# Gate and up of three feed-forwards as 2x2 block products, and both state-space builds in one phase

## The chip, the cores and the metric

One core of a Trainium2 chip runs the whole program. The metric is device time in microseconds, from the first to the last instruction of one execution. Engines are called PE (TensorE), DVE (VectorE), ACT (ScalarE), POOL (GpSimd) and SP (SyncE, which issues most DMAs).

## What is computed

Two layers of a decoder trunk on one sequence of 512 tokens with 1024 features, all in float32. A layer has four phases, in this order: a gated feed-forward (ffn1), three token mixers side by side (mix), cross-attention to 256 memory tokens (att), a second gated feed-forward (ffn2).

```python
def swiglu_ffn(h, w_gate, w_up, w_down):        # 1024 -> 2816 -> 1024
    return (jax.nn.silu(h @ w_gate) * (h @ w_up)) @ w_down

for l in range(2):
    x = x + 0.5 * swiglu_ffn(rmsnorm(x, ffn1_norm[l]), ...)
    z = rmsnorm(x, mix_norm[l]) @ w_in[l]
    y = concat(s5_mixer(z[:384], ...), pool_mixer(...), conv_module(...))
    x = x + y @ w_out[l]
    x = x + cross_attention(rmsnorm(x, xattn_norm[l]), rmsnorm(mem, mem_norm[l]), ...)
    x = x + 0.5 * swiglu_ffn(rmsnorm(x, ffn2_norm[l]), ...)
return rmsnorm(x, final_norm)
```

The s5 mixer is a state-space scan over 24 groups; its matrices (powers of a complex diagonal, input and output matrices, phase tables) come from the parameters alone, not from x.

## The kernel before

**Layout.** Activations are feature-major: `xs` holds x as 8 tiles of 128 features by 512 tokens. PE multiplies in float32r, and every operand is split in two float32r parts, a high one (`xh`, `wh`: an ACT copy) and a low one (`xl`, `wl`: a DVE subtraction of the high part from the original). `mm3` (lines 235 to 238) makes each product of three matmuls: high·high, high weight·low activation, low weight·high activation.

**Weights.** `wload` (lines 223 to 230) fetches a 128x1024 tile by a DMA on SP's queue, copies it to `wh` on ACT (L227) and subtracts on DVE (L229). Each of raw, `wh` and `wl` has three buffers in the pool `wp`.

**Feed-forward.** `ffn` (line 255) walks 22 blocks of 128 hidden features. `gate_up(f)` makes gate and up of one block, each 8 feature tiles times three matmuls of 512 columns into one PSUM bank, then gates: two DVE products read PSUM and the token scale `rb` (L269, L273), ACT makes the sigmoid, two DVE products read SBUF (L274, L275), and `split` halves the result (L243, L245). The blocks come in groups of 6, 6, 5, 5; `down(p)` adds a group into the 8 outputs, and stands behind the first block of the next group. In the last feed-forward the last group runs token-major, so that tiles are normalised and stored one by one.

**Norms.** `Norm.add(kt)` (line 185) follows each finished x tile: ACT makes the scaled high part and the square, DVE the low part and the running sum (L183, L189). The token scale `rb` is needed only when a block is gated.

**State-space matrices.** `s5_build(l)` (line 362) is a generator. Each ffn1 steps it once a block (`next(bg, None)`), so each layer's matrices are built beside that layer's first feed-forward. Its wide products and sums run on POOL, with a few matmuls and transposes on PE. The matrices stay in SBUF (pool `cp`) until the mixer of their layer.

**Order.** The code is traced in program order; a scheduler lays out each engine's instructions ahead of time, by program order among those which its timing model takes to be ready. On the chip each engine then runs its list in order. Buffers in a pool that come under one tag are shared, and an instruction that writes into one waits until its readers are done.

Of the kernel before, what the change touches and what calls it, by code (L numbers as in the profile page):

```python
# [9 lines left out]
F32 = mybir.dt.float32  # L10
F32R = mybir.dt.float32r
# [33 lines left out]
def trunk_kernel(ctx: ExitStack, tc: tile.TileContext, io, out, phases=None):  # L45
# [43 lines left out]
    def vt(name, shape=(P, 512), dt=F32):  # L89
        return vp.tile(list(shape), dt, tag="V", name=name)  # L90
# [107 lines left out]

    def rsqrt_cols(acc, scale, name, mark=None):
# [35 lines left out]
    def mm3(ps, wh, wl, ah, al, first, last):  # L235
        T.matmul(ps, lhsT=wh, rhs=ah, start=first, stop=False)  # L236
        T.matmul(ps, lhsT=wh, rhs=al, start=False, stop=False)  # L237
        T.matmul(ps, lhsT=wl, rhs=ah, start=False, stop=last)  # L238
# [14 lines left out]

# [1 line left out]
    def ffn(which, l, norm, nxt, bg):  # L255
        wg, wu, wd = (io[f"{which}_w_{n}"][l] for n in ("gate", "up", "down"))
        rb = norm.rb()
        sizes = [6, 6, 5, 5]
        starts = [0, 6, 12, 17]
        gs = {}  # L260

        def gate_up(f):
            nm = f"{which}{l}_{f}"
            pg = mm(f"pg{nm}")
            proj(pg, wg, 0, f * P, norm.xg, f"g{nm}", split_w=pre.pop("gate", None))
            pu = mm(f"pu{nm}")
            proj(pu, wu, 0, f * P, norm.xg, f"u{nm}", split_w=pre.pop("up", None))
            a = bt(f"a{nm}")
            V.tensor_tensor(out=a, in0=pg, in1=rb, op=MUL)  # L269
            s = bt(f"s{nm}")  # L270
            A.activation(out=s, in_=a, func=AF.Sigmoid)
            u = bt(f"u{nm}")
            V.tensor_tensor(out=u, in0=pu, in1=rb, op=MUL)  # L273
            V.tensor_tensor(out=a, in0=a, in1=s, op=MUL)  # L274
            V.tensor_tensor(out=a, in0=a, in1=u, op=MUL)  # L275
            gs[f] = split(a, f"ff{nm}")

        def down(p):
            f0, n = starts[p], sizes[p]
            last = p == len(sizes) - 1  # L280
            for o in range(NK):
                ps = mm(f"pd{which}{l}_{p}_{o}")
                proj(ps, wd, f0 * P, o * P, [gs[f0 + i] for i in range(n)], f"d{which}{l}_{p}_{o}")
                V.scalar_tensor_tensor(out=xs[o], in0=ps, scalar=0.5, in1=xs[o], op0=MUL, op1=ADD)  # L284
                if last:
                    nxt.add(o)

        # last block: token-major, so that each token tile is normalised and stored while the next is computed
        xt, wt = {}, []
        fl, nl = starts[-1], sizes[-1]  # L290
# [46 lines left out]
        gain = []  # L337
        for p, (f0, n) in enumerate(zip(starts, sizes)):
            for i in range(n):
                gate_up(f0 + i)  # L340
                if i == 0 and p > 0:
                    down(p - 1)
                if nxt is None and f0 == fl:
                    if i == 0:
                        for h in range(2):
                            gain.append(st(f"fgain{h}"))
                            nc.sync.dma_start(out=gain[h], in_=io["final_norm"][h * 512:(h + 1) * 512].partition_broadcast(P))
                    else:
                        to_tokens(i - 1)
                    fetch_rows(i)  # L350
                next(bg, None)
        for _ in bg:
            pass
        if nxt is None:
            finish()
        else:
            down(len(sizes) - 1)

# [1 line left out]
    s5m = {}  # L360

    def s5_build(l):
# [44 lines left out]
        # powers of lambda, ascending 1..8 (pm) and descending 7..0 (pg)  # L407
# [4 lines left out]
        # z = (lambda - 1) / lam  # L412
# [21 lines left out]
        # unit phase of one chunk  # L434
# [9 lines left out]
        # input matrix (hat = [re; im], til = [-im; re]) and its product with z  # L444
# [11 lines left out]
        G.tensor_tensor(out=bbh, in0=bh, in1=zrb, op=MUL)  # L456
        G.tensor_tensor(out=tmp, in0=btl, in1=zib, op=MUL)
        G.tensor_tensor(out=bbh, in0=bbh, in1=tmp, op=ADD)
        G.tensor_tensor(out=bbt, in0=btl, in1=zrb, op=MUL)
# [527 lines left out]
    for i, (kind, l) in enumerate(phases):  # L987
        nxt = norm_for(i + 1)
        if kind == "ffn1":
            def bg():  # L990
                if l == 0:
                    yield from prepare()
# [30 lines left out]
```

## Time and profile before

| what | value |
|---|---|
| median of 2 runs | 2139.3 us (2138.47 to 2140.12) |
| profiled execution, span | 2138.3 us, 25180 instructions |
| PE busy | 2088.5 us, 98%, 9685 matmuls |
| DVE, ACT, POOL busy | 1301.8 us (61%), 751.5 us (35%), 441.7 us (21%) |
| mean granted clock of PE | 0.991 |
| HBM | 203.32 MB read, 6.29 MB written, 98 GB/s |

The phases follow each other on PE; their borders, read from the chain that ended last: ffn1 of layer 0 until about 398 us, its mixer to 602, attention to 712, ffn2 to 1081; ffn1 of layer 1 until about 1454 us, mixer to 1657, attention to 1775, ffn2 to the end. Matmuls are pipelined, so the duration of one (0.39 us for 512 columns) is longer than the distance at which the next one starts. "Idle before" in a row is the engine's idle time ahead of those instructions, with what ended it.

### The profile page before, as it was taken

The page shows a single profiled execution, that of the slowest core. Times are in us where ns is not written, and L with a number is a line of the kernel's source. Part 1 is how long each engine was busy: PE and PEld are TensorE (multiplying, and loading weights), DVE is VectorE, ACT ScalarE, POOL GpSimd, SP SyncE. Part 2 cuts the span into 40 slices and gives each one's busy share as a digit, 9 for nine tenths or more (in the row PEclk, how much of TensorE's full clock was granted, in tenths as well). Part 3 has the DMA queues.
Part 4 walks back from the last instruction along what each step waited for, and adds up shares of the span by engine and source line. Part 5 has one row for each costly group of instructions (what it writes and reads, how often), then busy time and mean ns, then how long its engine had stood idle before and what let it go on. Part 6 is the DMA issues. An engine that isn't in the chain of part 4 may idle for free.

```text
span 2138.3 us, 25180 instructions
## 1 busy us (share of the span) xinstructions
PE 2088.5 (98%) x9685; PEld 1733.4 (81%) x9685; DVE 1301.8 (61%) x1942; ACT 751.5 (35%) x1060; POOL 441.7 (21%) x477
## 2 busy tenths in 40 slices
PE   8999999989999999999999999999989999999998
PEld 6888888877787888888887888887868878888887
DVE  7766454699755544444577564456996655454454
ACT  4423222434434322222352323233344443222232
POOL 2217170457000000000013680006550000000000
PEclk9999999989999999999999999999999999999999
DMA  5342332444322323333333333334443323333241
GB/s 168 98 125 75 115 98 73 133 125 132 98 80 58 91 85 112 88 94 105 89 95 93 104 96 99 103 89 128 125 124 89 89 59 94 94 96 101 80 147 40
DMA packets 396256, 213.03 MB, mean 100 GB/s; under 512 B 31934, under 2 KB 387048, under 8 KB 396136
## 3 DMA queue, kind: packets, MB, share of 16 engines
q1 hardware_dynamic: 395344, 210.32, 33.8%
q8 instruction: 76, 1.25, 0.3%
q10 hardware_dynamic: 792, 1.10, 0.1%
q14 instruction: 44, 0.36, 0.1%
HBM read 203.32 MB, written 6.29 MB: 98 GB/s over the span
## 4 chain that ended last, share of the span: by engine, by line
PE 86%; DVE 10%; issue 1%; DMA 1%; ACT 1%; SPq 0%; POOL 0%; POOLq 0%; DVEq 0%; ACTq 0%
PE pgffn L236 7%; PE pgffn L237 7%; PE pgffn L238 7%; PE puffn L237 7%; PE puffn L238 7%; PE puffn L236 7%; PE pdffn L238 7%; PE pdffn L236 7%; PE pdffn L237 7%; DVE cacc L727 3%; PE qps L237 1%; PE po L236 1%; PE qps L236 1%; PE po L238 1%; PE pwo L236 1%
## 5 line engine op out<-in xcount | busy, mean ns | idle before, releaser
L236 PE MATMUL pgffn<-xh_ffn,wh_gffn 128*128 128x512 f32 x696 | 272.6, 392 | 0.0
L237 PE MATMUL puffn<-xl_ffn,wh_uffn 128*128 128x512 f32 x696 | 272.2, 391 | 0.0
L238 PE MATMUL puffn<-xh_ffn,wl_uffn 128*128 128x512 f32 x696 | 271.9, 391 | 0.0
L236 PE MATMUL puffn<-xh_ffn,wh_uffn 128*128 128x512 f32 x696 | 271.6, 390 | 0.0
L237 PE MATMUL pgffn<-xl_ffn,wh_gffn 128*128 128x512 f32 x696 | 271.4, 390 | 0.0
L238 PE MATMUL pgffn<-xh_ffn,wl_gffn 128*128 128x512 f32 x696 | 271.3, 390 | 0.0
L238 PE MATMUL pdffn<-h_ffffn,wl_dffn 128*128 128x512 f32 x664 | 257.9, 389 | 0.9 <-DVE wl_dffn L229 0.9
L237 PE MATMUL pdffn<-l_ffffn,wh_dffn 128*128 128x512 f32 x664 | 258.3, 389 | 0.0
L236 PE MATMUL pdffn<-h_ffffn,wh_dffn 128*128 128x512 f32 x664 | 257.8, 389 | 0.0
L227 ACT ACTIVATE wh_dffn<-wr_dffn 128x768 fp32r<-128x768 f32 (+1 forms) x120 | 94.9, 795 | 286.9 <-PE pdffn L237 148.3
L284 DVE SCALAR_TENSOR_TENSOR x<-pdffn,x 128x512 f32<-128x512 f32 x120 | 82.4, 689 | 168.7 <-PE pdffn L238 168.6
L273 DVE TENSOR_TENSOR uffn<-puffn,rb_ffn 128x512 f32<-128x512 f32 x88 | 60.7, 690 | 197.8 <-PE puffn L238 197.8
L227 ACT ACTIVATE wh_uffn<-wr_uffn 128x1024 fp32r<-128x1024 f32 x87 | 92.2, 1060 | 250.7 <-PE pgffn L237 155.2
L227 ACT ACTIVATE wh_gffn<-wr_gffn 128x1024 fp32r<-128x1024 f32 x87 | 92.2, 1060 | 249.5 <-issue 154.7
L269 DVE TENSOR_TENSOR affn<-pgffn,rb_ffn 128x512 f32<-128x512 f32 x88 | 60.7, 690 | 164.8 <-PE pgffn L238 158.6
L236 PEld LDWEIGHTS puffn<-xh_ffn,wh_uffn 128*128 128x128 f32 x696 | 131.0, 188 | 27.4 <-issue 0.2
L237 PEld LDWEIGHTS puffn<-xl_ffn,wh_uffn 128*128 128x128 f32 x696 | 131.0, 188 | 27.5 <-issue 0.2
L238 PEld LDWEIGHTS puffn<-xh_ffn,wl_uffn 128*128 128x128 f32 x696 | 131.0, 188 | 27.0
L238 PEld LDWEIGHTS pgffn<-xh_ffn,wl_gffn 128*128 128x128 f32 x696 | 130.7, 188 | 27.3
L237 PEld LDWEIGHTS pgffn<-xl_ffn,wh_gffn 128*128 128x128 f32 x696 | 130.8, 188 | 26.6
L236 PEld LDWEIGHTS pgffn<-xh_ffn,wh_gffn 128*128 128x128 f32 x696 | 130.7, 188 | 26.5
L238 PEld LDWEIGHTS pdffn<-h_ffffn,wl_dffn 128*128 128x128 f32 x664 | 124.6, 188 | 27.2 <-DVE wl_dffn L229 1.3
(456 smaller groups left out, 4197.4 us busy)
## 6 DMA issues: line engine op xcount, KB each, us to landing
wr_gffn<-in_ffn_w_gate_dram SPq DMA_DIRECT2D x87, 512.0 KB
wr_uffn<-in_ffn_w_up_dram SPq DMA_DIRECT2D x87, 512.0 KB
wr_dffn<-in_ffn_w_down_dram SPq DMA_DIRECT2D x64, 384.0 KB
wr_dffn<-in_ffn_w_down_dram SPq DMA_DIRECT2D x56, 320.0 KB
wr_k<-in_xattn_wk_dram SPq DMA_DIRECT2D x16, 512.0 KB
wr_v<-in_xattn_wv_dram SPq DMA_DIRECT2D x16, 512.0 KB
wr_wo<-in_w_out_dram SPq DMA_DIRECT2D x16, 512.0 KB
wr_q<-in_xattn_wq_dram SPq DMA_DIRECT2D x16, 512.0 KB
```

The costliest lines, as they stand in the source:

```text
L227: A.activation(out=h, in_=raw, func=AF.Copy)
L236: T.matmul(ps, lhsT=wh, rhs=ah, start=first, stop=False)
L237: T.matmul(ps, lhsT=wh, rhs=al, start=False, stop=False)
L238: T.matmul(ps, lhsT=wl, rhs=ah, start=False, stop=last)
L269: V.tensor_tensor(out=a, in0=pg, in1=rb, op=MUL)
L273: V.tensor_tensor(out=u, in0=pu, in1=rb, op=MUL)
L284: V.scalar_tensor_tensor(out=xs[o], in0=ps, scalar=0.5, in1=xs[o], op0=MUL, op1=ADD)
L727: V.scalar_tensor_tensor(out=acc[:, d:], in0=h[:, 0:S - d], scalar=cw[:, TAPS - 1 - d:TAPS - d], in1=acc[:, d:], op0=MUL, op1=ADD)
```

## The change

Three of the four feed-forwards (ffn2 of layer 0, ffn1 and ffn2 of layer 1) use a new function, `ffn7`. It takes two blocks of hidden features as a pair. Weights [2 halves of the features x 2 blocks] times activations [2 halves of the features x 2 halves of the tokens] is a product of 2x2 block matrices, made by seven block products instead of eight, with sums of blocks ahead and behind. A block product is 4 feature tiles times gate and up (z) times three matmuls, of 256 columns.

- Activation sums are made in the norm ahead (`PairNorm`, `combos`), each split in high and low, for two x tiles 512 features apart; the phases ahead finish x tiles in the order 0, 4, 1, 5, 2, 6, 3, 7.
- Weight sums (four a pair, 128x1024) are made on POOL (`wsum`), then split by `halves`.
- Three PSUM banks (x, y, z) collect; partial results are copied out (`keep`, ACT) or added (`out`, DVE) between products.
- `gated` works on both blocks of a pair, from SBUF, and is spread over the products that follow (`later`).
- `pipeline` writes the order: loads seven steps ahead, weight sums four, halves two. Groups are 6, 6, 6, 4 blocks.

The first feed-forward keeps `ffn`, and steps the background twice a block: it now builds the matrices of both layers. Layer 0 builds on POOL and keeps them in SBUF; layer 1 builds on DVE, spills them to DRAM, and its mixer loads them back. The small pools are merged into one of 53 buffers.

```diff
+    class PairNorm(Norm):
+        def add(self, kt):
+            self.sums(kt)
+            self.done.add(kt)
+            k = kt % HK
+            if {k, k + HK} <= self.done:
+                self.pair(k)
+        def pair(self, k):
+            xa = ct_(f"xa_{self.name}{k}", (P, 4, HS))
+            for h in range(2):
+                A.activation(out=xa[:, 2 * h:2 * h + 2, :], in_=xs[k + h * HK].rearrange("p (h t) -> p h t", t=HS),
+                             func=AF.Identity, scale=self.col(k + h * HK))
+            self.xg[k] = combos(xa, f"{self.name}{k}")
+    def combos(xa, name):
+        V.tensor_tensor(out=s1, in0=xa[:, 3, :], in1=xa[:, 1, :], op=SUB)
+        V.tensor_tensor(out=s3, in0=xa[:, 0, :], in1=xa[:, 1, :], op=SUB)
+        V.scalar_tensor_tensor(out=s2, in0=s1, scalar=-1.0, in1=xa[:, 0, :], op0=MUL, op1=SUB)
+        V.scalar_tensor_tensor(out=s4, in0=xa[:, 2, :], scalar=-1.0, in1=s2, op0=MUL, op1=SUB)
...
+    def halves(src, name, shape):
+        h = wp.tile(list(shape), F32R, tag="wh", name=f"wh_{name}")
+        A.activation(out=h, in_=src, func=AF.Copy)
+        lo = wp.tile(list(shape), F32R, tag="wl", name=f"wl_{name}")
+        V.tensor_tensor(out=lo, in0=src, in1=h.bitcast(F32), op=SUB)
+        return h, lo
+    def pipeline(steps, later, bg, per):
+        for i in range(-7, n):
+            if 0 <= i + 7 < n and steps[i + 7].load:
+                steps[i + 7].load()
+            if 0 <= i + 4 < n and steps[i + 4].mix:
+                steps[i + 4].mix()
+            if 0 <= i + 2 < n:
+                w[i + 2] = steps[i + 2].split()
...
+            while steps[i].after and later:
+                later.pop(0)()
+            steps[i].run(w.pop(i))
+            if steps[i].post:
+                steps[i].post()
+            if later:
+                later.pop(0)()
...
+    def ffn7(which, l, norm, nxt):
+        sizes = [6, 6, 6, 4]
+        def pair(f):
+            def load(kh, fh):
+                r = (ct_(f"wr_{nm}_{kh}{fh}", shape) if (kh, fh) == (0, 1) else
+                     wp.tile(list(shape), F32, tag="raw", name=f"wr_{nm}_{kh}{fh}"))
+                for z, w in enumerate((wg, wu)):
+                    nc.sync.dma_start(out=r[:, z], in_=w[...])
+            def wsum(i, a, b):
+                ts[i] = ct_(f"wt_{nm}_{i}", shape)
+                G.tensor_tensor(out=ts[i], in0=a, in1=b, op=ADD)
+            def run(c, i, first):
+                    for k in range(HK):
+                        xh, xl = norm.xg[k][i]
+                        for z in range(2):
+                            mm3(ps[c][:, z, :], w[0][:, z, k, :], w[1][:, z, k, :], xh, xl, first and k == 0 and z == 0,
+                                k == HK - 1, True)
+            def one():
+                    V.scalar_tensor_tensor(out=g, in0=g, scalar=sgn, in1=rb, op0=MUL, op1=MUL)
+                    A.activation(out=sg[0], in_=g, func=AF.Sigmoid)
+                    V.scalar_tensor_tensor(out=u, in0=u, scalar=sgn, in1=rb, op0=MUL, op1=MUL)
+            def two():
+                    V.tensor_tensor(out=g, in0=g, in1=sg[0], op=MUL)
+                    V.tensor_tensor(out=g, in0=g, in1=u, op=MUL)
+                    gs[f + b] = split(g, f"ff{nm}_{b}")
...
+            add("x", 1, True, lambda: raw[0, 0], lambda: keep("x", "u1"), lambda: load(0, 0))
+            add("z", 5, True, lambda: ts[5], lambda: keep("z", "u5"), lambda: load(0, 1),
+                lambda: wsum(5, raw[0, 0], raw[0, 1]))
+            add("x", 6, False, lambda: ts[6], lambda: keep("x", "u2"), lambda: load(1, 1),
+                lambda: (wsum(7, raw[1, 1], raw[0, 1]), wsum(6, ts[7], raw[0, 0])))
+            add("z", 3, False, lambda: raw[1, 1], lambda: out(1, 0, "z", "u2"))
+            add("x", 7, False, lambda: ts[7], lambda: out(1, 1, "x", "u5"), lambda: load(1, 0))
+            add("y", 2, True, lambda: raw[1, 0], lambda: out(0, 0, "y", "u1"))
+            add("x", 4, False, lambda: ts[4], last_post, None, lambda: wsum(4, ts[6], raw[1, 0]))
...
-    def s5_build(l):
+    def s5_build(l, kept):
+        E = G if kept else V
...
-                G.tensor_tensor(out=gt, in0=bc_m(bbh), in1=bc_p(pg, 0), op=MUL)
+                E.tensor_tensor(out=gt, in0=bc_m(bbh), in1=bc_p(pg, 0), op=MUL)
...
+        mats, rho, spill = s5m.pop(l)
+        if spill is not None:
+            for f in range(NS):
+                for i in range(len(MATS)):
+                    nc.sync.dma_start(out=mats[f][i], in_=spill[f][i])
...
-        for o in range(NK):
+        for o in (0, 4, 1, 5, 2, 6, 3, 7):
             ps = mm(f"pwo{l}_{o}")
```

## Rows read from the trace of the kernel before

**Rows 1.** The page: busy time of PE; the chain that ended last, by engine.
```profile
PE 2088.5 (98%) x9685; PEld 1733.4 (81%) x9685; DVE 1301.8 (61%) x1942; ACT 751.5 (35%) x1060; POOL 441.7 (21%) x477
...
PE 86%; DVE 10%; issue 1%; DMA 1%; ACT 1%; SPq 0%; POOL 0%; POOLq 0%; DVEq 0%; ACTq 0%
```
**Rows 2.** Busy time by stage; the first line names the columns.
```profile
core 0: us, PE busy (x) PEld busy (x) DVE busy (x) ACT busy (x) POOL busy (x), PEclk, DMA share, GB/s
...
398.00:570.00 172.00, 159.34 (x816) 132.91 (x815) 146.71 (x206) 68.41 (x92) 87.80 (x51) 0.94 0.39 117
712.00:1075.00 363.00, 363.00 (x1611) 300.79 (x1610) 184.83 (x237) 111.06 (x141) 1.01 (x1) 1.00 0.33 96
1090.00:1447.00 357.00, 354.79 (x1599) 293.77 (x1599) 218.95 (x354) 121.86 (x166) 118.82 (x174) 1.00 0.33 96
```
**Rows 3.** PE's waits over the span: who for whom, us, times, longest.
```profile
PE yps L681 <- DVE sy L677: 10.9, 4, 4.1
...
PE cps L474 <- DMA cn<-in_ssm_c_im_dram: 2.2, 1, 2.2
...
PE pdffn L238 <- DVE wl_dffn L229: 0.9, 1, 0.9
```
**Rows 4.** PE's timeline (start, duration), first and last of 24, 512 columns.
```profile
799.68 0.39 PE L238 MATMUL pdffn<-h_ffffn,wl_dffn 128*128 128x512 f32 x1
...
804.90 0.39 PE L237 MATMUL pdffn<-l_ffffn,wh_dffn 128*128 128x512 f32 x1
```
**Rows 5.** The same, first and last of 35, 256 columns.
```profile
1538.81 0.28 PE L238 MATMUL kps<-mg,wl_k 128*128 128x256 f32 x1
...
1542.89 0.28 PE L236 MATMUL kps<-mg,wh_k 128*128 128x256 f32 x1
```
**Rows 6.** DVE's groups by line and shape, 725 to 1075 us (busy, mean ns).
```profile
L229 DVE TENSOR_TENSOR wl_gffn<-wr_gffn,wh_gffn 128x1024 fp32r<-128x1024 f32 x22 | 26.8, 1220 | 4.1 <-ACT wh_gffn L227 4.1
...
L284 DVE SCALAR_TENSOR_TENSOR x<-pdffn,x 128x512 f32<-128x512 f32 x32 | 22.0, 690 | 50.9 <-PE pdffn L238 50.9
L229 DVE TENSOR_TENSOR wl_dffn<-wr_dffn,wh_dffn 128x768 fp32r<-128x768 f32 x16 | 15.3, 959 | 0.1
...
L275 DVE TENSOR_TENSOR affn<-affn,uffn 128x512 f32<-128x512 f32 x22 | 15.2, 690 | 0.5
L245 DVE TENSOR_TENSOR l_ffffn<-affn,h_ffffn 128x512 fp32r<-128x512 f32 x22 | 15.1, 688 | 7.0 <-ACT h_ffffn L243 7.0
```
**Rows 7.** ACT's groups, the same stretch.
```profile
L227 ACT ACTIVATE wh_gffn<-wr_gffn 128x1024 fp32r<-128x1024 f32 x21 | 22.3, 1062 | 66.1 <-issue 47.8 <-PE pdffn L237 17.5 <-ACT sq_ffn L179 0.5
...
L243 ACT ACTIVATE h_ffffn<-affn 128x512 fp32r<-128x512 f32 x22 | 13.9, 634 | 22.9 <-DVE affn L275 22.9
L271 ACT ACTIVATE sffn<-affn 128x512 f32<-128x512 f32 x22 | 13.6, 619 | 0.5 <-DVE affn L269 0.3
```
**Rows 8.** Timelines of POOL and DVE, 456 to 464 and 200 to 235 us.
```profile
458.37 2.37 POOL L229 TENSOR_TENSOR wl_k<-wr_k,wh_k 128x1024 fp32r<-128x1024 f32 x1
...
458.55 2.72 DVE L667 TENSOR_TENSOR sy<-sy,ssw 128x512 f32<-128x512 f32 x1
...
201.91 5.08 DVE L229 TENSOR_TENSOR wl_dffn<-wr_dffn,wh_dffn 128x768 fp32r<-128x768 f32 x1
...
202.02 0.46 POOL L545 TENSOR_TENSOR tab<-tab,ta 128x128 f32<-128x128 f32 x1
...
205.44 0.73 POOL L545 TENSOR_TENSOR tab<-tab,ta 128x256 f32<-128x256 f32 x1
```
**Rows 9.** DVE's groups, 1090 to 1440 us, while POOL builds.
```profile
L229 DVE TENSOR_TENSOR wl_gffn<-wr_gffn,wh_gffn 128x1024 fp32r<-128x1024 f32 x19 | 26.6, 1402 | 1.0 <-ACT wh_gffn L227 1.0
...
L229 DVE TENSOR_TENSOR wl_dffn<-wr_dffn,wh_dffn 128x768 fp32r<-128x768 f32 x16 | 22.0, 1372 | 0.1
...
L245 DVE TENSOR_TENSOR l_ffffn<-affn,h_ffffn 128x512 fp32r<-128x512 f32 x22 | 20.1, 915 | 5.8 <-ACT h_ffffn L243 5.8
```
**Rows 10.** POOL's groups, the same stretch.
```profile
L519 POOL TENSOR_TENSOR mout<-mout,mtt 128x512 f32<-128x512 f32 x6 | 10.9, 1842 | 0.0
...
L500 POOL TENSOR_TENSOR gt<-bbh,pg 128x512 f32<-128x512 f32 x6 | 7.6, 1272 | 41.0 <-PE vps L507 40.9
```

More of the change, by code (lines that the diff above doesn't have):

```diff
@@ L252, in proj @@
             mm3(ps, h[:, k, :], lo[:, k, :], ah, al, k == 0, k == n - 1)
[L255 to L280, printed above, removed]
-            for o in range(NK):
[L282 to L290, printed above, removed]
@@ new lines, in halves, with __init__ @@
+    def halves(src, name, shape):
+        h = wp.tile(list(shape), F32R, tag="wh", name=f"wh_{name}")
+        A.activation(out=h, in_=src, func=AF.Copy)
+        lo = wp.tile(list(shape), F32R, tag="wl", name=f"wl_{name}")
+        V.tensor_tensor(out=lo, in0=src, in1=h.bitcast(F32), op=SUB)
+        return h, lo
+    class Step:
+        def __init__(self, run, split, post=None, load=None, mix=None, after=False):
+            self.run, self.split, self.post, self.load, self.mix, self.after = run, split, post, load, mix, after
@@ new lines, in pipeline @@
+    def pipeline(steps, later, bg, per):
+        n = len(steps)
+        w = {}
+        for i in range(-7, n):
[5 more added lines that the diff above has]
+                w[i + 2] = steps[i + 2].split()
+            if i < 0:
+                continue
+            while steps[i].after and later:
[5 more added lines that the diff above has]
+                later.pop(0)()
+            for _ in range(per):
+                next(bg, None)
+        while later:
+            later.pop(0)()
+        for _ in bg:
+            pass
@@ L342, in ffn @@
                     down(p - 1)
[L343 to L351, printed above, removed]
+                for _ in range(2):
+                    next(bg, None)
@@ L484, in s5_build, with whole, half, put @@
         vsb = st(f"vsb{l}", (P, NG, GK))
+        def whole(name, shape):
+            return ct_(f"{name}{l}_{f}", shape) if kept else None
+        def half(tile_, sl, name, shape):
+            return sl(tile_) if kept else st(f"{name}{l}_{f}", shape)
+        def put(i, sl, t):
+            if not kept:
+                nc.sync.dma_start(out=sl(spill[f][i]), in_=t)
+        spill = None if kept else [[drp.tile(list(shape), F32, tag=f"m{f}{i}", bufs=1, name=f"sm{l}_{f}{i}")
+                                    for i, shape in enumerate(MATS)] for f in range(NS)]
         for f in range(NS):
-            minT = ct_(f"minT{l}_{f}", (P, GF, P))
+            minT = whole("minT", MATS[0])
             vps = ax(f"vps{l}_{f}", (P, GF, GK))
@@ L908, in attention @@
         out_head(NH - 1)
-        for o in range(NK):
+        for o in (0, 4, 1, 5, 2, 6, 3, 7):
             ps = mm(f"pwo{l}_{o}")
@@ L973, in norm_for, with seven @@
         kind, l = phases[i]
-        return Norm(f"{kind}{l}", lambda k: pc(gains[kind], l, k), G if i == 0 else V)
+        col = lambda k: pc(gains[kind], l, k)
+        if seven(i):
+            return PairNorm(f"{kind}{l}", col)
+        return Norm(f"{kind}{l}", col, G if i == 0 else V)
+    def seven(i):
+        return i > 0 and phases[i][0] in ("ffn1", "ffn2")
     cur = norm_for(0)
@@ L990, in bg @@
             def bg():
-                if l == 0:
+                if i == 0:
                     yield from prepare()
-                yield from s5_build(l)
-            ffn("ffn1", l, cur, nxt, bg())
+                    for k in range(L):
+                        yield from s5_build(k, k == 0)
+            if seven(i):
+                ffn7(kind, l, cur, nxt)
+            else:
+                ffn(kind, l, cur, nxt, bg())
         elif kind == "mix":
```

234 lines of the change are left out of this document (185 added, 49 removed).

## The prediction

> **What bounds the kernel now.** I read the page first. PE is busy 98% of the span and carries 86% of the chain that ended last [rows 1]. A busy PE need not be PE at its peak, so I asked for stages next. Through the last 363 us up to 1075 us, a whole feed-forward, PE is never idle, at a granted clock of 1.00 (the 2.4 GHz level), with VectorE (DVE) at 184.8 us and GpSimd (POOL) at 1.0 us. Layer 1's first feed-forward, in which the state-space matrices are built, has POOL at 118.8 us and DVE at 219.0 us, and PE idle for 2.2 us of 357 [rows 2]. The list of PE's waits agrees: in all feed-forwards one wait on a weight half (0.9 us) and one on a DMA (2.2 us); the long waits are the mixers' [rows 3], and there the granted clock falls to 0.94 [rows 2]. So in the feed-forwards only fewer PE columns, or a cheaper column, can shorten the run, and only while nobody else becomes later than PE.
>
> **PE's side of the change.** The price of a matmul is the distance between starts, not the duration. In steady runs 24 matmuls of 512 columns start 5.22 us apart, first to last: 0.227 us each [rows 4]. 35 matmuls of 256 columns with a new 128x128 weight each, as the change has them, start 4.08 us apart: 0.120 us each [rows 5]. Half the columns cost 53%, not 50%. Two blocks of gate and up took 2·2·8·3 = 96 matmuls of 512: 21.8 us. Seven products of 4·2·3 = 24 matmuls of 256 are 168: 20.2 us. That is 1.63 us less a pair; 11 pairs in each of three feed-forwards give 33·1.63 = **-53.8 us**. The down projections keep their columns. The Trainium skill ("TensorE: Matmul & The Clock Gate", Back-to-back issue gap) gives N/2.4 + 2.5 ns, 216 and 109 ns; by that the gain would be an estimated 33·2.37 = 78 us. Both rows here lie 11 ns above it, so its sum is not used.
>
> **What DVE, ACT and POOL get in exchange, per pair.** Prices are those of the stage in which POOL rests [rows 6, 7].
> - DVE: seven weight halves of 128x1024 at 1.22 instead of four: 8.5 us. Gating reads two SBUF tiles in all five steps for each of two blocks: 10·0.69 = 6.9 us (before, two of the five read PSUM). Three output sums of PSUM and SBUF: 3·0.69 = 2.1 us. Together 17.5 us in a pair that takes PE 20.2.
> - ACT: seven halves at 1.06, four PSUM copies, two sigmoids and two splits at 0.62 to 0.63: 12.4 us. It stays free.
> - POOL: four sums of two 128x1024 tiles. The nearest row, a two-input POOL instruction of that size, is 2.37 us [rows 8]: 9.5 us. POOL had nothing here before.
>
> DVE alone fits, with 2.7 us to spare. The question is whether DVE and POOL run beside each other. [rows 8] say no when the DVE instruction has two SBUF inputs: such a 0.69 us instruction, issued 0.18 us after a POOL sum, takes 2.72 us and ends after the sum does; elsewhere one of 0.96 us takes 5.08 us, through a chain of POOL instructions. Then a pair needs 8.5 + 6.9 + 9.5 = 24.9 us one after the other, and about 1.3 of the 2.1 us of PSUM sums that don't fall under a POOL sum: **26.3 us against PE's 20.2**, an excess of 6.1 wherever pair follows pair. The DVE halves are made two products ahead of PE, so PE waits for them; before, a pair was 21.8. By the Trainium skill ("SBUF — State Buffer", Who interferes with whom) the pair of ports is held for a whole instruction, which is this reading.
>
> The other reading is an average. In layer 1's first feed-forward 118.8 us of POOL lengthened the DVE's two-input work by about 22·0.18 + 16·0.41 + 66·0.21 = 24 us [rows 9], 0.2 us per us. By that a pair costs DVE 17.5 + 1.9 = 19.4 us and PE never waits. I don't take it: there two-input DVE work was about 120 us and POOL 119 us in 350 us, so they fitted beside each other in time. 24.9 us in 20.2 can't.
>
> **Where the excess lands.** A 6-block down projection is 8·18·0.227 = 32.7 us of PE and asks DVE for 8·(0.96 + 0.69) = 13.2 us and POOL for nothing. It can take the gating of the pair ahead of it (6.9 us), and in its last steps two halves and three POOL sums of the pair behind it (9.6 us), as the loads are issued seven products ahead. The order in a feed-forward is four pairs, down, three pairs, down, three pairs, down, one pair, down.
> - Four pairs: 4·6.1 = 24.5; less 6.9 and 9.6: 8.0. Bounds: 4.3 (all PSUM sums hidden and more prefetched) to 17.6 (nothing prefetched).
> - Three pairs, twice: 18.4 - 16.5 = 1.9 each (bounds 1.8 to 11.5).
> - The last pair: its excess is prefetched; but its last gating (about 5 us of DVE and ACT in turn) must end before the last down block; PE has 9 matmuls of three ready blocks for each of two outputs, 4 us: 2 (0 to 6).
> Sum 13.8 a feed-forward, three of them: **+41.4 us**.
>
> **The norm before a seven-product feed-forward.** For two feature tiles DVE now makes four sums, four low halves and two square sums, at most 0.69 each, some of half width: 5.6 us for two outputs. After attention two outputs are 2·8·3·0.227 = 10.9 us of PE against 9.4 us of DVE with weight halves and residual: only the last pair is late, 3 us, bounds 0 to 6. After the second feed-forward, whose last down has 4 blocks, two outputs are 5.4 us of PE against 8.4 us of DVE, four times: 12 less what PE can take from later products, 9, bounds 3 to 13. Attention twice and feed-forward once: **+15 us**. Before, PE didn't wait there at all [rows 2].
>
> **Both builds in the first feed-forward.** The matmuls, loads and small DVE steps only move. Layer 0's build stays on POOL at twice the rate per block. Layer 1's goes to DVE: 36 products and sums of 128x512 that took POOL 1.3 to 1.8 us [rows 10] take 0.69, 25 us; the other 66 us of POOL's 118.8 I put at half, 33 us (bounds 20 and 66). It is spread over 6 blocks of two background steps each: 9.7 us a block on top of the old 2·1.22 + 5·0.69 = 5.9, against 10.9 us of PE. Four blocks in a row have no down between them: 4·4.7 = 19, less weight halves made ahead and work that slides into the next down: **+10 us** (0 to 25). Its results go to DRAM and come back, 3 MB, ahead of the layer 1 mixer's weights on the SP queue; they can start while the last down runs: **+2** (0 to 8). The wait on the DMA in layer 1 goes: **-2.2** [rows 3].
>
> **Sum against the profiled execution:** 2138.3 - 53.8 + 41.4 + 15 + 10 + 2 - 2.2 = 2150.7. The median of the runs is 1.0 above the profile: **2152 us**.
>
> **The rivals.**
> - *PE's sum stands.* If the average reading holds, or the scheduler's order lets gating slide into the downs, the boundary and build terms vanish with it: 2139.3 - 53.8 - 2.2 = 2083. For it: PE has not one long wait in the feed-forwards now. Against: [rows 8]. It needs the whole added wait under 11 us.
> - *Nothing is made ahead.* One mechanism, on the other side: the raw weight tiles have three buffers, shared by pair and down, and SP's loads are in order. If the next pair's loads queue behind the down's, its POOL sums begin with its first product and block DVE just then; each stretch loses its 9.6 us again (6 for the last pair). 3·(3·9.6 + 6) = 104 us in full, 2256; with half of it, 2204. From the point where 30 us of the 104 are lost it is slower by 2%. Behind DVE's blocked half stand the output sums that free PE's accumulators, so PE would wait twice. For it: the pair's second load goes to another pool, its others don't; against: DMA is at a third [rows 2].
> - *ACT or DMA becomes the bound.* 12.4 of 20.2 us, and the weight bytes per us grow by 8%: I give it nothing.
>
> **Chances.** Ports in turn, with down as the relief: 0.51, 2152, its own range 2107 (low bounds) to 2182. PE's sum: 0.17, 2083. Nothing made ahead, half to all: 0.32, 2204 and up. The range must reach into both: 2083 to 2210 leaves out the upper part of the last. Two per cent, 43 us, is about what a measurement of this kernel can tell from no change: faster (under 2096) 0.17, the same 0.51, slower (over 2182) 0.32.
>
> **What the new profile would show.** Right: the 256-column products start 0.120 us apart inside a product and PE waits for `wl` halves on DVE at the ends of products, most in the first four pairs of a feed-forward; DVE's 128x1024 halves average well over 1.22 us there, and POOL's sums over 2.4; DVE and POOL together fill the pair stretches; the down stretches have no PE waits. A pair takes about 26 us in the middle of the first four. Wrong: pairs at 20.2 us with DVE halves near 1.3 (PE's sum), or PE waits in every pair behind a down too (nothing made ahead). If the products themselves start farther apart than 0.120 us, or the first feed-forward takes over 25 us longer than before, the error is in those terms.

## The result and the profile after

Median 2270.2 us (2 runs, 2269.3 to 2271.2), against 2139.3: a ratio of 1.061 (95% interval 1.0579 to 1.0641), 131 us slower. The forecast was no change that can be told, at 2152.

The page of the changed kernel, busy time of PE and the chain that ended last; they answer to [rows 1]:

```profile
PE 2081.9 (92%) x12061; PEld 1829.9 (81%) x12061; DVE 1690.0 (74%) x2376; ACT 929.0 (41%) x1331; POOL 720.9 (32%) x444
...
PE 57%; DVE 23%; issue 15%; ACT 2%; POOL 1%; DMA 1%; SPq 0%; DVEq 0%; POOLq 0%; ACTq 0%
```

Of the chain's "issue" (time in which the engine waited for nothing that the profile shows), 347 us, 222 lie in the two attention phases, whose length didn't change.

PE's busy time hardly fell: 2088.5 to 2081.9, 6.6 us, where 53.8 of work were taken away. Its idle time rose from 49.8 to 187.5 (span less busy). So there are two losses: waits (137.7 us more), and 47 us in which PE is busy without more work. The forecast had only waits, 68 us, half of those that came. Where they lie, by stage. The lines answer to [rows 2] and are cut at the last output matmul of each phase: first feed-forward, first mixer, feed-forward 2 of layer 0, feed-forward 1 of layer 1, attention of layer 1, the last feed-forward.

```profile
core 0: us, PE busy (x) PEld busy (x) DVE busy (x) ACT busy (x) POOL busy (x), PEclk, DMA share, GB/s
0.00:436.90 436.90, 399.32 (x1814) 326.44 (x1815) 309.51 (x716) 152.98 (x226) 126.91 (x197) 0.97 0.40 116
436.90:661.40 224.50, 191.81 (x945) 158.46 (x944) 165.51 (x234) 82.27 (x114) 91.87 (x53) 0.91 0.35 106
780.50:1160.00 379.50, 352.65 (x2406) 327.82 (x2404) 301.84 (x317) 170.39 (x230) 140.98 (x47) 0.98 0.32 92
1160.00:1536.30 376.30, 352.91 (x2380) 327.66 (x2381) 299.28 (x312) 164.78 (x219) 127.05 (x46) 0.97 0.35 107
1761.20:1880.40 119.20, 116.60 (x579) 97.71 (x578) 72.40 (x131) 54.02 (x102) 1.01 (x1) 1.00 0.25 72
1880.40:2269.30 388.90, 360.06 (x2424) 335.04 (x2423) 294.39 (x305) 167.49 (x228) 137.97 (x49) 0.97 0.30 90
```

Every stage has PE idle, attention only 2.6 us (2.3 before), and every stage but attention has a granted clock under 1.00. Phase by phase, by the same cuts in both traces:

| phase | before | after | change |
|---|---|---|---|
| first feed-forward | 391.1 | 436.9 | +45.8 |
| mixers, layer 0 and 1 | 201.4, 201.3 | 224.5, 224.9 | +46.7 |
| attention, twice | 119.3, 119.4 | 119.2, 119.2 | 0 |
| ffn2 of layer 0 and ffn1 of layer 1 | 734.7 | 755.8 | +21.1 |
| last feed-forward, to its last output | 364.5 | 382.3 | +17.8 |

PE's waits, which answer to [rows 3] (who for whom, us, times, longest). `wl_guffn` is the low half of a gate and up weight, `xm` a negated activation sum, `prm` and `affn` belong to the first feed-forward, `lsm` and `pq` to the mixers:

```profile
PE pxffn L281 <- DVE wl_guffn L302: 37.3, 23, 2.7
PE lmean L983 <- DVE lsm L981: 29.9, 2, 15.4
PE ppo L867 <- DVE pq L863: 18.1, 4, 7.8
PE pdffn L279 <- DVE affn L407: 8.2, 1, 8.2
...
PE pxffn L279 <- ACT xm_ffn L230: 5.9, 1, 5.9
PE puffn L279 <- DVE prm L651: 5.7, 1, 5.7
PE pdffn L281 <- DVE wl_dffn L272: 5.6, 1, 5.6
...
PE pxffn L280 <- DVE xm_ffn L231: 5.2, 1, 5.2
```

The first row is the wait that the prediction named, but not in the place that it named: the longest twelve of these waits, 1.91 to 2.70 us each, all stand at the first product of a pair. The mixers' two, 48 us, it didn't have at all. DVE's groups and then POOL's, 780 to 1536 us, which answer to [rows 6]:

```profile
L302 DVE TENSOR_TENSOR wl_guffn<-wt_ffn,wh_guffn 128x1024 fp32r<-128x1024 f32 x88 | 141.6, 1609 | 22.7 <-ACT wh_guffn L300 22.3
...
L494 DVE SCALAR_TENSOR_TENSOR guffn<-guffn,rb_ffn 128x512 f32<-128x512 f32 x44 | 54.4, 1235 | 0.7
```

```profile
L462 POOL TENSOR_TENSOR wt_ffn<-wr_ffn,wr_ffn 128x1024 f32<-128x1024 f32 x44 | 134.4, 3059 | 415.3 <-DMA wr_ffn<-in_ffn_w_up_dram 408.1 <-DVE l_ffffn L288 5.9 <-ACT u5ffn L477 1.2
L462 POOL TENSOR_TENSOR wt_ffn<-wt_ffn,wr_ffn 128x1024 f32<-128x1024 f32 x44 | 128.1, 2911 | 14.1 <-DMA wr_ffn<-in_ffn_w_up_dram 9.4 <-ACT wh_guffn L300 1.7
```

A half takes 1.61 us instead of 1.22, a gating step 1.24 instead of 0.69, a POOL sum about 3.0 instead of 2.37. How they lengthen each other is seen in the timelines of DVE and POOL (start, duration):

```profile
826.59 0.68 DVE L484 TENSOR_TENSOR guffn<-pzffn,u2ffn 128x512 f32<-128x512 f32 x1
827.19 2.82 DVE L302 TENSOR_TENSOR wl_guffn<-wt_ffn,wh_guffn 128x1024 fp32r<-128x1024 f32 x1
829.93 0.68 DVE L484 TENSOR_TENSOR guffn<-pxffn,u5ffn 128x512 f32<-128x512 f32 x1
830.65 2.18 DVE L494 SCALAR_TENSOR_TENSOR guffn<-guffn,rb_ffn 128x512 f32<-128x512 f32 x1
```

```profile
825.64 3.29 POOL L462 TENSOR_TENSOR wt_ffn<-wr_ffn,wr_ffn 128x1024 f32<-128x1024 f32 x1 [5.94 <-DVE l_ffffn L288]
829.01 6.09 POOL L462 TENSOR_TENSOR wt_ffn<-wt_ffn,wr_ffn 128x1024 f32<-128x1024 f32 x2
```

The half that starts at 827.19 gets nowhere until POOL's sum ends at 828.93, and then needs 1.1 us. The two sums with a PSUM input (0.68) pass beside POOL's sums unhindered. The gating step with two SBUF inputs waits again. This is the reading of [rows 8] that the prediction chose; the Trainium skill ("SBUF — State Buffer", Who interferes with whom) says that a DVE instruction with two SBUF inputs contends with a POOL instruction that reads SBUF, and calls the ports that they share an exclusive lock. These rows agree.

### The profile page after: what moved, and what is told of

Its sections match the earlier page's. It is cut to its first block, busy times and chain, and to the rows that moved or that the text cites. A ratio compares the mean times of both kernels' runs of the same rounds, so it can differ in the third digit from the quotient of the medians.

```text
span 2269.4 us, 31369 instructions
## 1 busy us (share of the span) xinstructions
PE 2081.9 (92%) x12061; PEld 1829.9 (81%) x12061; DVE 1690.0 (74%) x2376; ACT 929.0 (41%) x1331; POOL 720.9 (32%) x444
## 3 DMA queue, kind: packets, MB, share of 16 engines
q1 hardware_dynamic: 408896, 222.91, 33.1%
## 4 chain that ended last, share of the span: by engine, by line
PE 57%; DVE 23%; issue 15%; ACT 2%; POOL 1%; DMA 1%; SPq 0%; DVEq 0%; POOLq 0%; ACTq 0%
PE pdffn L279 6%; PE pdffn L281 6%; PE pdffn L280 6%; DVE wl_guffn L302 6%; DVE cacc L970 4%; PE pxffn L281 4%; PE pxffn L280 3%; PE pxffn L279 3%; PE pzffn L279 2%; PE pzffn L280 2%; PE pzffn L281 2%; PE pgffn L281 2%; PE pgffn L279 2%; PE pgffn L280 2%; PE puffn L279 1%
## 5 line engine op out<-in xcount | busy, mean ns | idle before, releaser
L462 POOL TENSOR_TENSOR wt_ffn<-wr_ffn,wr_ffn 128x1024 f32<-128x1024 f32 x66 | 203.7, 3091 | 601.5 <-DMA wr_ffn<-in_ffn_w_up_dram 587.4
L302 DVE TENSOR_TENSOR wl_guffn<-wt_ffn,wh_guffn 128x1024 fp32r<-128x1024 f32 x132 | 213.4, 1616 | 35.9 <-ACT wh_guffn L300 35.2
L281 PE MATMUL pxffn<-xh_ffn,wl_guffn 128*128 128x256 f32 x792 | 224.5, 284 | 2.3 <-DVE wl_guffn L302 2.3
L279 PE MATMUL pxffn<-xh_ffn,wh_guffn 128*128 128x256 f32 x792 | 224.9, 284 | 1.7 <-ACT u1ffn L477 1.4
L280 PE MATMUL pxffn<-xl_ffn,wh_guffn 128*128 128x256 f32 x792 | 224.3, 283 | 0.0
L462 POOL TENSOR_TENSOR wt_ffn<-wt_ffn,wr_ffn 128x1024 f32<-128x1024 f32 x66 | 192.4, 2915 | 19.3 <-DMA wr_ffn<-in_ffn_w_up_dram 13.1
L302 DVE TENSOR_TENSOR wl_guffn<-wr_ffn,wh_guffn 128x1024 fp32r<-128x1024 f32 x99 | 158.8, 1604 | 33.1 <-ACT wh_guffn L300 33.0
L279 PE MATMUL pzffn<-xh_ffn,wh_guffn 128*128 128x256 f32 x528 | 153.5, 291 | 8.2 <-ACT wh_guffn L300 4.5
L281 PE MATMUL pzffn<-xh_ffn,wl_guffn 128*128 128x256 f32 x528 | 152.3, 288 | 3.1 <-DVE wl_guffn L302 3.0
L281 PEld LDWEIGHTS pdffn<-h_ffffn,wl_dffn 128*128 128x128 f32 x672 | 127.1, 189 | 33.9 <-DVE wl_dffn L272 6.4
L280 PE MATMUL pzffn<-xl_ffn,wh_guffn 128*128 128x256 f32 x528 | 152.2, 288 | 0.0
```

Of the source, the lines that this page charges most:

```text
L279: T.matmul(ps, lhsT=wh, rhs=ah, start=first, stop=False, skip_group_check=skip)
L280: T.matmul(ps, lhsT=wh, rhs=al, start=False, stop=False, skip_group_check=skip)
L281: T.matmul(ps, lhsT=wl, rhs=ah, start=False, stop=last, skip_group_check=skip)
L302: V.tensor_tensor(out=lo, in0=src, in1=h.bitcast(F32), op=SUB)
L462: G.tensor_tensor(out=ts[i], in0=a, in1=b, op=ADD)
```

## The experiments

"Mixers" are always the lengths of layer 0 and layer 1; each run has its own runs of the kernel before beside it (2139.4 to 2139.7).

### Is it the pool, the builds or the feed-forwards?

**b_pool**: the kernel before, its three small pools merged as in the change, nothing else.

```diff
-    bp = ctx.enter_context(tc.tile_pool(name="bp", bufs=36))
-    vp = ctx.enter_context(tc.tile_pool(name="vp", bufs=4))
+    bp = ctx.enter_context(tc.tile_pool(name="bp", bufs=53))
-    ssp = ctx.enter_context(tc.tile_pool(name="ssp", bufs=13))
...
-        return vp.tile(list(shape), dt, tag="V", name=name)
+        return bt(name, shape, dt)
...
-        return ssp.tile(list(shape), dt, tag="S", name=name)
+        return bt(name, shape, dt)
```

> The kernel before, with its three pools of 36, 4 and 13 buffers merged into one of 53, and nothing else of the change. After the change each mixer took 23 us longer, in layer 0 too, where nothing of the mixer's code was changed. Theory M (the merged pool): the scheduler gives the mixer's state-space inputs their buffers later, and lists them behind convolution taps; then both mixers are 15 to 30 us longer here, 2170 to 2200 us in all, with the feed-forwards as before or a few us worse. Rival R (what the change does around the mixers, the spill or the norms): the mixers take 201 us as before, 2139 us. Where the first feed-forward also gets longer here, the pool has a part in that term too.

Measured: 2189.3 us, ratio 1.0231 (1.0201 to 1.0261). Mixers 225.6 and 224.2, the first feed-forward 389.2. That is the first theory's range: 50 us of the 131 come from lines without any arithmetic in them.

**b_build**: the kernel before, pools apart, with both builds in the first feed-forward, two steps a block, layer 1's on DVE and spilled, as in the change.

```diff
-                yield from s5_build(l)
+                    for k in range(L):
+                        yield from s5_build(k, k == 0)
...
-                next(bg, None)
+                for _ in range(2):
+                    next(bg, None)
```

> The kernel before, its pools apart as they were, with both layers' matrices built in the first feed-forward (two background steps a block, layer 1 on DVE, spilled and loaded back), and no seven-product feed-forward. Theory B (the builds): the first feed-forward becomes about 46 us longer, of which some 13 are matmuls that only move from layer 1's first feed-forward, which becomes shorter by that; the sum is +25 to +35, 2165 to 2175 us. Rival (the merged pool made the first feed-forward late): +13 there and -13 in layer 1, 2139 us within 8. The spill's load shows in the layer 1 mixer against that of layer 0: 0 to 8 us.

Measured: 2146.4 us, ratio 1.0033 (1.0021 to 1.0046). First feed-forward 407.0, +15.9; ffn2 and ffn1 of layer 1 721.9, -12.8, so most of it is work that moved, as the rival had it. Mixer of layer 1, which loads the spilled matrices, 202.1 against layer 0's 202.8: with the pools apart the loads cost nothing.

**b_poolbuild**: both edits together.

> The kernel before with both changes that b_pool and b_build made singly: one pool of 53 buffers, and both layers' matrices built in the first feed-forward; no seven-product feed-forward. Those two gave +50 and +7 us. If the terms only add, 2195 us, with the first feed-forward at 405 to 409 us. If they need each other (the builds' tiles and the feed-forward's now take buffers from one another), the first feed-forward is at 430 to 440 us as in the changed kernel, and the time 2215 to 2230. What is left to the changed kernel's 2270 us is the seven-product feed-forwards' own.

Measured: 2222.7 us, ratio 1.0384 (1.0354 to 1.0414). That is 83 us, 26 more than the two alone (50 and 7). The first feed-forward alone is 31 us longer than with the builds and the pools apart, 438.1 instead of 407.0; other phases give a little back. Layer 1's mixer takes 228.6 here, against 223.1 for layer 0's. Two windows of this kernel in that stretch, columns as above:

```profile
80.00:130.00 50.00, 30.77 (x118) 23.84 (x117) 43.19 (x146) 12.97 (x24) 27.30 (x35) 0.80 0.21 50
130.00:180.00 50.00, 45.01 (x207) 37.04 (x206) 32.09 (x26) 14.31 (x21) 39.40 (x77) 0.93 0.30 87
```

With the pools apart the same windows have PE busy 43.87 and 50.00 us. The changed kernel's are 31.77 and 44.37, the same loss. What remains for the seven-product feed-forwards is 2270.2 - 2222.7 = 48 us.

### Which of the merged pools?

**b_v** merges only the state-space tiles (tag S, 13 buffers) into the big pool; V, which holds the gated convolution inputs `ca` and `ch`, stays apart. **b_s** is the mirror.

```diff
-    bp = ctx.enter_context(tc.tile_pool(name="bp", bufs=36))
+    bp = ctx.enter_context(tc.tile_pool(name="bp", bufs=49))
-    ssp = ctx.enter_context(tc.tile_pool(name="ssp", bufs=13))
...
-        return ssp.tile(list(shape), dt, tag="S", name=name)
+        return bt(name, shape, dt)
```

> The kernel before, with the 13 small state-space buffers (tag S) merged into the big pool, 49 in all, and the 4 value buffers (tag V) left apart. Merging both cost 50 us, all in the two mixers (225.6 and 224.2 us against 201). Theory: it is the V tiles that do the harm. In the pool of one tag a value tile can take any buffer, and the scheduler then lets the value products and the pool mixer run ahead of the state-space scaling su; with 4 apart they can't. Then this run keeps both mixers near 203 us and takes about 2142. Rival: the S tiles do it, their quick turnover among 13 is lost and the chain su, yps waits for buffers held by long-lived B tiles. Then the mixers stay near 225 and the run takes about 2185. Halfway (mixers near 215, about 2165) would mean both.

> The mirror of the run with V apart: the kernel before, V merged into the big pool (40), the 13 S buffers apart. If V does the harm: mixers near 225 us, about 2185. If S does it: mixers near 203, about 2142. If each alone costs nothing and only the two together do, both runs come out near 2142.

Measured: b_v 2173.1 us (1.0122 to 1.0181), mixers 216.7 and 218.3; b_s 2157.7 (1.005 to 1.0109), mixers 211.5 and 210.1. Neither theory: each half costs, 33 and 18 us, and 51 together against b_pool's 50. Where, is read from two tiles in layer 0's mixer: `su`, the state-space input, and `lsm`, the sum of the convolution's outputs (count, duration in ns min/median/max, first and last start). First the kernel before, then b_v, then b_s:

```profile
L585 DVE TENSOR_TENSOR su<-psu,rb_mix x3: 1128/1134/1139, 425.4 to 438.1; 128x512 f32<-128x512 f32 x3
...
L738 DVE TENSOR_TENSOR lsm<-lsm,cv x1: 680/680/680, 545.1 to 545.1; 128x512 f32<-128x512 f32 x1
```

```profile
L584 DVE TENSOR_TENSOR su<-psu,rb_mix x3: 1108/1140/1142, 457.9 to 466.8; 128x512 f32<-128x512 f32 x3
...
L737 DVE TENSOR_TENSOR lsm<-lsm,cv x1: 693/693/693, 543.6 to 543.6; 128x512 f32<-128x512 f32 x1
```

```profile
L584 DVE TENSOR_TENSOR su<-psu,rb_mix x3: 1064/1125/1169, 423.1 to 436.7; 128x512 f32<-128x512 f32 x3
...
L737 DVE TENSOR_TENSOR lsm<-lsm,cv x1: 693/693/693, 551.6 to 551.6; 128x512 f32<-128x512 f32 x1
```

Merging S makes the state-space chain 29 us later and leaves the convolution; merging V makes the convolution 6.5 us later and leaves the state space. In b_pool both are late (454.1 and 564.6). DVE's work in layer 0's mixer is the same before and after, 167.3 and 165.5 us: only the order differs. Which buffer's release moves an instruction back was not separated.

**a_v4**: the changed kernel with V's four buffers apart again (49 and 4).

> The changed kernel with the four buffers for the mixer's convolution inputs and the attention's probabilities apart again (49 and 4 in place of 53). Theory: with one pool, the inputs of the second and third convolution tile find no buffer until the pooling mixes have freed theirs, so their matmuls stand behind the pooling's in PE's list; then the mixers go back to 201 to 207 us, and the time to 2225 to 2238. If the 13 buffers of the state-space tiles were what counted, the mixers stay over 220 us.

Measured: 2251.0 us, 19 less than the change, mixers 218.7 and 216.2. Neither branch came (201 to 207, or over 220): V's four buffers are a part of it, and the rest stays, as b_v has it.

**a_ssmfirst**: the changed kernel with the state-space input traced ahead of the pool mixer.

```diff
-        for i in range(NPL):
-            pool_mix(i)
         for f in range(NS):
             ssm_in(f)
+        for i in range(NPL):
+            pool_mix(i)
```

> The changed kernel with one block of the mixer moved: the state-space inputs are traced ahead of the pooling mixes, so that they ask for their buffers first. Theory M: both mixers lose most of their extra 23 us, 2225 to 2250 us in all. If buffers are not what makes the state-space inputs late, the mixers stay at 224 us and the time at 2270.

Measured: 2264.6 us, mixers 222.4 and 221.6. Written order alone gives back 6 us. The last scaling `su` of layer 0's mixer starts at 483.0 instead of 503.3 us, but the pool mixer's last `pq` then comes 13 us later (509.3), and the last `lsm`, for which PE waits 17.0 us there, is as late as before (611.0 against 611.3). The merged pool isn't mended by moving one step.

### What do the weight sums cost the feed-forwards?

**a_nosum**: the changed kernel in which each weight sum is replaced by one of its raw blocks; PE, ACT and DVE do as much as before.

```diff
-                ts[i] = ct_(f"wt_{nm}_{i}", shape)
-                G.tensor_tensor(out=ts[i], in0=a, in1=b, op=ADD)
+                ts[i] = b
```

> The changed kernel without POOL's weight sums: each product takes one of the raw blocks in place of the sum, so those products are not of the reference. Theory P (POOL's sums and DVE's two-input instructions take turns at the ports): the DVE weight halves fall from 1.61 to about 1.22 us, a pair that follows a pair takes 20.2 to 20.8 us instead of 22.3 to 23.4, and the three feed-forwards lose 40 to 70 us of waits in all; the boundary behind an x tile's norm shrinks too; 2200 to 2230 us. Rival (DVE's own load of 17.5 us a pair, or the accumulators' copies, hold PE): pairs stay over 22 us and the time over 2255.

Measured: 2192.0 us, 78 less than the change. ffn2 and ffn1 709.6, last feed-forward 349.2: 46.2 and 33.1 less, more than the 40 to 70 expected. DVE's half in its groups, 780 to 1490 us:

```profile
L302 DVE TENSOR_TENSOR wl_guffn<-wr_ffn,wh_guffn 128x1024 fp32r<-128x1024 f32 x153 | 186.8, 1222 | 78.1 <-ACT wh_guffn L300 76.4 <-DMA wr_ffn<-in_ffn_w_up_dram 1.7
```

1.22 us again. PE's timeline of a stretch of three pairs, its first matmul and the first of the down projection behind it; the change first, with the starts of its second and third pair, then this run:

```profile
912.92 0.28 PE L279 MATMUL pxffn<-xm_ffn,wh_guffn 128*128 128x256 f32 x1
...
933.07 0.28 PE L279 MATMUL pxffn<-xm_ffn,wh_guffn 128*128 128x256 f32 x1
...
954.32 0.28 PE L279 MATMUL pxffn<-xm_ffn,wh_guffn 128*128 128x256 f32 x1
...
977.43 0.40 PE L279 MATMUL pdffn<-h_ffffn,wh_dffn 128*128 128x512 f32 x1
```

```profile
899.76 0.28 PE L279 MATMUL pxffn<-xm_ffn,wh_guffn 128*128 128x256 f32 x1
...
960.24 0.40 PE L279 MATMUL pdffn<-h_ffffn,wh_dffn 128*128 128x512 f32 x1
```

60.5 us without sums: exactly three pairs at 168 times 0.120. With sums the pairs take 20.2, 21.3 and 23.1. All stretches, read in this way:

| stretch | PE's work | with sums | without |
|---|---|---|---|
| four pairs, in ffn2, ffn1, ffn2 | 80.6 | 99.9, 107.0, 102.6 | 84.8, 97.4, 84.8 |
| three pairs, six times | 60.5 | 64.5, 66.1, 66.1, 66.7, 66.2, 66.3 | 60.4 to 60.5 |
| the down projections between | 32.7 | 32.6 to 32.7 | 32.6 to 32.7 |

**a_dvesum**: the same sums, made on DVE.

```diff
-                G.tensor_tensor(out=ts[i], in0=a, in1=b, op=ADD)
+                V.tensor_tensor(out=ts[i], in0=a, in1=b, op=ADD)
```

> The changed kernel with the weight sums on DVE in place of POOL. Theory P (turns at the ports): a sum then costs DVE about 1.22 us in place of 2.4 to 3 us of POOL during which DVE's two-input instructions stand still; a pair asks DVE for 17.5 + 4.9 = 22.4 us, and pairs behind pairs take 22 to 23 us, pairs behind a down 20.2; the seven-product feed-forwards get 15 to 45 us shorter in all, 2225 to 2255 us. Rival (PE waits because a sum is late, whoever makes it, and DVE's list is full): no shorter, 2265 us or more.

Measured: 2243.5 us, 27 less than on POOL; in the feed-forwards 16.2 and 14.7 less.

```profile
L302 DVE TENSOR_TENSOR wl_guffn<-wt_ffn,wh_guffn 128x1024 fp32r<-128x1024 f32 x88 | 107.2, 1218 | 14.6 <-ACT wh_guffn L300 14.5
...
L462 DVE TENSOR_TENSOR wt_ffn<-wt_ffn,wr_ffn 128x1024 f32<-128x1024 f32 x44 | 53.5, 1215 | 0.2
```

Four more instructions of 1.22 us a pair on the busiest helper are cheaper than the same work on a resting engine: a pair then has 17.5 + 4.9 = 22.4 us in a row instead of 24.9, and in the middle of a stretch pairs start 21.7 us apart (PE's products come in a slightly different order there, too). The busy times by the page:

```profile
PE 2078.1 (93%) x12061; PEld 1824.0 (81%) x12061; DVE 1665.3 (74%) x2508; ACT 935.5 (42%) x1331; POOL 323.7 (14%) x312
```

DVE runs 132 instructions more than in the change and is busy 24.7 us less. With a_nosum's 1222 ns this puts the place at the ports. The rival, that a sum is late whoever makes it, fails in the change's own trace too: the twelve longest waits stand before a product of a raw block, which needs no sum, and ahead of the one that ends at 1054.72 DVE has no idle time for 17 us.

### The first feed-forward, and all repairs together

**a_rate**: the changed kernel, background at one step a block for ten blocks, then three.

```diff
-                for _ in range(2):
+                for _ in range(1 if f0 + i < 10 else 3):
                     next(bg, None)
```

> The changed kernel with the background stepped once a block in the first ten blocks of the first feed-forward and three times in the rest, in place of twice in all. The waits there stand at 84 to 145 us, in layer 0's build. If two steps a block of layer 0's build on POOL are their cause, the first feed-forward falls from 437 to 408 to 418 us and the time to 2240 to 2252. If the merged pool's buffers are, it stays over 428 us, or the waits move to the later blocks.

Measured: 2260.5 us, 10 less, the first feed-forward 423.4 instead of 436.9, between the two branches (418, 428); layer 0's mixer is 4 us longer. Its windows where the change lost most:

```profile
80.00:130.00 50.00, 50.00 (x224) 41.01 (x224) 39.83 (x162) 18.11 (x25) 2.42 (x7) 1.00 0.34 102
130.00:180.00 50.00, 50.00 (x231) 41.36 (x230) 31.10 (x30) 17.83 (x29) 28.72 (x34) 1.00 0.41 108
```

PE is full there now. What lengthens DVE's row in the change is seen in its timeline, the build's tiny products (24 elements a partition), and in POOL's, whose build steps follow each other there without a gap:

```profile
116.73 0.17 DVE L621 TENSOR_TENSOR prm<-prm 128x24 f32<-128x24 f32 x1
116.84 1.06 DVE L616 TENSOR_TENSOR prm<-prm 128x24 f32<-128x24 f32 x1
...
119.02 1.24 DVE L620 TENSOR_TENSOR ph<-prm 128x24 f32<-128x24 f32 x1
```

```profile
116.73 2.23 POOL L751 TENSOR_TENSOR mtt<-ctil,pm 128x512 f32<-128x512 f32 x2
118.92 2.55 POOL L752 TENSOR_TENSOR mout<-mout,mtt 128x512 f32<-128x512 f32 x2
```

An instruction of 0.17 us takes 1.1 to 1.2, and such a chain stands ahead of `affn`, for which PE waits 8.2 us. Before the wait of 5.6 us two halves `wl_dffn`, 0.96 us each alone, take 10.57 us together under POOL's chain. That isn't the whole cause: with the pools apart (b_build) the tiny products of 80 to 150 us last 27.8 us against 36.5, and PE has one wait there, 6.1 us. What else the merged pool puts ahead of `affn` was not separated.

**a_best**: the changed kernel with a_v4, a_dvesum and a_rate at once.

> The changed kernel with three repairs at once: value buffers apart (alone -19 us), weight sums on DVE instead of POOL (alone -27), and the background at one step a block in the first ten blocks, three after (alone -10). If the three act in different stretches (mixers; seven-product feed-forwards; first feed-forward), they add up: 2270.2 - 19.3 - 26.7 - 9.7 = about 2215, with PE idle near 145 us instead of 187.5. If they share one cause (buffers of the merged pool), less than the sum: 2225 to 2240. Either way it stays above the kernel before, 2139, since the sums still cost DVE 1.2 us each and the first feed-forward still builds twice.

Measured: 2212.3 us, ratio 1.0335 (1.0305 to 1.0365); first feed-forward 421.3, mixers 219.3 and 219.7. The three gains add up (58.0 against 55.7), as separate causes would. PE's idle time is 124.6 us by the trace, less than the 145 expected. It is still 73 us slower than the kernel before. No variant of the change that was run beats the kernel before; seven-product feed-forwards with all pools apart were not tried.

## Why the prediction was wrong

**PE's saving: right.** 0.120 us a matmul inside a product, 60.5 us for three pairs, so -53.8 stands. The formula of the Trainium skill ("TensorE: Matmul & The Clock Gate", Back-to-back issue gap), 109 ns, is given there for an isolated matmul; this stream lies above it, so the prediction was right not to use it.

**The sum.** The forecast missed by 118 us. Two steps failed most: the merged pool was put at nothing, and the relief in the pair stretches was too large. By the terms below, in us: the merged pool in the mixers 47, the builds 23, the pair stretches 40, the norm boundaries 10, less 2 for the spill. The last pair's 2 us held: PE waits 1.6 us for its gating in each of the first two seven-product feed-forwards.

**The merged pool: a term that was missing.** The change's description has the line, the sum gave it nothing. It cost 46.7 us in the two mixers, two fifths of the error, and 31 in the first feed-forward by way of the builds (438.1 against 407.0).

**Both builds: +10 in the forecast, 33 in the run** (45.8 less the 12.8 that left layer 1's feed-forward). The prediction's own sign for it, over 25 us longer, came. The place was wrong too. The prediction put it on layer 1's build on DVE in the late blocks; there PE is full but for 3.3 us from 230 to 437. It is layer 0's build, at 80 to 180 us. With the pools apart and the same builds the net cost is 3 (15.9 less 12.8), so the price of moving them was not the error; the pool was. The spill's +2 was 0 there.

**The pair stretches: mechanism right, size wrong.** From the table: with less without sums, the four-pair stretches lost 15.1, 9.6 and 17.8, predicted 8.0 each; the six three-pair stretches 4.0 to 6.2, 33 in all, predicted 1.9 each. Together 75 against 35. The step that failed is the relief: pairs took 20.2, 21.3, 23.1, so one pair behind a down is free, and the next two pay. The relief of 16.5 us a stretch was summed up as if DVE could spend it anywhere. And pairs behind pairs took 20.7 to 24.6 us, not 26.3: the excess for each was too high, the number of pairs that pay too low. One reason for the first is that DVE was priced by durations, not by the distance between starts, as PE was. With POOL at rest DVE's steps start 0.60 us apart where they last 0.68 (at 933.89, 934.50 and 935.10 us) and 1.13 where a half lasts 1.21 (935.10, then 936.23). By these starts the 24.9 us are an estimated 7.9 + 6.0 + 9.5 = 23.4. The lower clock, below, is part of the 75.

**The norm boundaries: +15 in the forecast, 25 measured.** Without sums the four-pair stretches exceed PE's work by 4.2, 16.8 and 4.2 (predicted 3, 9, 3). Behind attention the step held within 1.2 us; between two feed-forwards it was half of what came, and in the changed kernel PE waits there for `xm` twice, 5.9 and 5.2 us.

**PE's clock: not priced.** ffn2 and ffn1 should have had PE busy for 721.8 us (b_poolbuild) less 35.9; they had 705.6, 19.7 more; the last feed-forward in the same way 13.4 more. Windows and a timeline show the larger part. The first window lies behind one wait of 2.70 us; the other two, and the timeline, behind another of 2.70 us:

```profile
957.40:960.60 3.20, 3.18 (x26) 3.18 (x27) 3.20 (x5) 0.37 (x1) 0.00 (x0) 1.00 0.44 121
1054.70:1057.90 3.20, 3.18 (x15) 3.18 (x16) 3.20 (x5) 0.00 (x0) 0.00 (x0) 0.50 0.41 123
1058.10:1061.80 3.70, 3.70 (x33) 3.70 (x33) 3.56 (x5) 2.59 (x4) 0.00 (x0) 1.00 0.00 0
```

```profile
1054.72 0.58 PE L281 MATMUL pxffn<-xm_ffn,wl_guffn 128*128 128x256 f32 x1 [2.70 <-DVE wl_guffn L302]
...
1055.32 0.41 PE L280 MATMUL pxffn<-xm_ffn,wh_guffn 128*128 128x256 f32 x1
1055.53 0.41 PE L281 MATMUL pxffn<-xm_ffn,wl_guffn 128*128 128x256 f32 x1
```

Behind the wait that ends at 1054.72 the next 15 matmuls start 0.21 us apart at the 1.2 GHz level, then 0.12 at 2.4 again: it cost 1.4 us more. The equal wait that ends at 957.42 cost nothing more, at a granted clock of 1.00. Of the twelve waits of 1.91 to 2.70 us seven were followed by matmuls at the lower level and five weren't; what decides it, these runs don't show. [rows 2] had the sign of it, a granted clock of 0.94 where the mixer waits, and the prediction didn't turn it into a price. For the three feed-forwards over b_poolbuild: PE's work -53.8, idle time +72.1 (50.2 and 21.9), busy time beyond the work +33.1. That adds up to the 51.4 by which the two stages grew (33.9 and 17.5), by definition, as the 33.1 is what is left. Of it the lower clock is about 21: half of PE's busy time while the trace has the clock at 0.50. About 9 more is no slower work: at each of 54 waits the matmul ahead is busy for 0.28 us, where the next would have started after 0.12.

**The rivals.** "PE's sum stands" is out: the halves took 1.61 us, as [rows 8] had said. "Nothing is made ahead" gives the right sign by a wrong cause: the first pair behind each down takes PE's 20.2 us, so its weights were made ahead. Its mark, more than 30 us over the forecast, was passed by the pool, which no rival held, and by the later pairs of each stretch. The low end of the forecast's own range, 2107, comes to 2110 by the bounds that it names.

## To carry to other kernels

Price every line of a diff, buffers too: a pool with a tag of its own also sets the order, and merging three cost 50 us with no engine's work changed. Work given to a resting POOL isn't free when DVE is at 80% of the stage with two-input operations; ask what DVE and POOL need one after the other, and credit a relief only to the next instructions, not to the whole stretch. Price DVE, like PE, by the distance between starts. And give a wait of PE a range: its length, and the slower matmuls that may follow it.

## What the runs showed that was not expected

- Small DVE instructions suffer much beside POOL in proportion: 0.17 us becomes 1.06 to 1.24.
- A wait of 2.7 us could be followed by 3.2 us at the lower clock, or by none. Over the run PE is busy for 101 us at the lower level, against 34 before, and half of that is lost: 33 us more.
- Sums of 1.22 us on DVE, at 74% busy, beat the same sums on POOL, at 32%, by 27 us, and DVE's busy time fell.
